# Six of eight output projection tiles per layer as pairs of tiles in seven block products

## The chip, the cores and the metric

The kernel runs on one core of a Trainium2 chip. The metric is device time in microseconds (us) of one execution. The engines are named as in the profile: PE (TensorE, matmuls), PEld (its weight loads), DVE (VectorE), ACT (ScalarE), POOL (GpSimd) and SP (SyncE, which issues nearly all DMAs here). "L996" is line 996 of the kernel before.

## What is computed

The reference is a trunk of two layers over 16 learned meta tokens and 512 sequence tokens (528 in all), 1024 features wide, in float32. One layer is:

```
h = rmsnorm(x)
u_pool, z_pool, c_q, c_kv, k_rope, z_mla, g_pool, g_mla = split(h @ w_in)
y_pool = (pool_mix(u_pool) * silu(z_pool)) @ pool_w_up
y_mla  = (mla(c_q, c_kv, k_rope) * silu(z_mla)) @ mla_w_up
merged = sigmoid(g_pool) * y_pool + sigmoid(g_mla) * y_mla
x = x + merged @ w_out
```

`mla` is latent attention with eight heads, with query blocks of 128 tokens. The output is x without the meta positions. The change touches the last line, `merged @ w_out`, a product of 1024 x 1024 weights with 528 tokens (512 in the last layer).

## The kernel before, in words

Features lie on the 128 partitions and tokens along the columns. Every projection is cut into tiles of 128 output features. A tile is a `Gemm` in the list `plan`; `register` (L1007) writes that list by hand, layer by layer, and `stream` (L190) walks through it as a generator. The layer's own code (`go`, and the attention code in `head`, `prep` and `pv`) draws from that generator in small steps, so that matmuls of the projections fill the gaps of the attention. `after(LAG, fn)` puts a piece of work some modelled nanoseconds later into the stream. The Tile framework then places the instructions of every engine in an order of its own, by their order of emission and by what it holds to be ready, and each engine runs its list in order. So a DMA that is emitted later may stand ahead of an earlier one that has to wait.

Precision is kept by splitting: each float32 operand becomes a high part and a low part in the matmul's own format, and `mm3` (L180) issues three matmuls, high by high, high by low and low by high (L181 to L183). A weight chunk of 512 columns (four blocks of 128 input features for one output tile) is fetched by `fetch` (L114) into `raw`, its high part is made by ACT (L176) and its low part by DVE (L177) in `wload`. There are three buffers each for `raw`, `whi` and `wlo`; a Gemm marked `spare` takes two buffers `th` and `tl` of another pool instead. The stream asks for one chunk ahead of the one it multiplies.

The stretch around the change, in each layer:

- `pu` and `gp` leave the gated pool branch in `am[m]`, which lies in `xb[:, m]`.
- `mu0` to `mu7` are the up-projection of the attention branch, 12 matmuls per chunk of columns. Their evacuation `ev_mu` (L975) takes the PSUM result times the gate into a `tmp` (DVE, L980), adds `am[m]` (POOL, L982) and splits the sum into `mg[m]`, high part on ACT (L275), low part on DVE (L276). `mg[m]` uses the buffers of `h` (`hh`, `hl`).
- `o0` to `o7` are the output projection: for each tile two weight chunks of four input blocks each. `ev_o` (L986) fetches the residual (L990 or L993), adds half of the PSUM result to it (DVE, L996) and stores it (L1000 or L1002); in layer 0 it also squares the new x for the next layer's norm (`square_x`: ACT L347, sums on POOL L351).

Layer 0 works on all 528 tokens in two halves of 264 columns (`FULL`), layer 1 on the 512 sequence tokens in one piece (`XTOK`), but for its last tile, which is cut into halves of 256. PSUM has four tiles `mm`, three `S` and one `o`. The residual tiles `tmp` have three buffers.

Of the kernel before, what the change touches and what calls it, by code (L numbers as in the profile page):

```python
# [71 lines left out]
def trunk(ctx, tc, xT, xrow, mrow, pos, win, wkr, wqb, wkb, wvb, wgr, wpu, wmu, wout, gains, const, yT):  # L72
# [13 lines left out]
    def nm(s):  # L86
        uid[0] += 1
        return f"{s}_{uid[0]}"
# [73 lines left out]
    class Gemm:  # L162
        def __init__(self, name, src, width, evac=None, xs=None, segs=None, body=None):
            self.name, self.src, self.width, self.alloc = name, src, width, mmt
            self.evac, self.xs, self.segs, self.body = evac, xs, segs, body
            self.spare = False

    loads = [0]

    def wload(src, n, spare):  # L170
        raw = early.pop(0) if early else fetch(src, n, rawt(), sp)
        loads[0] += 1
        pool, th, tl, nb = (tp, "th", "tl", 2) if loads[0] <= 2 or spare else (wp, "whi", "wlo", 3)
        hi = pool.tile([P, W if pool is tp else 512], F32R, tag=th, name=nm("whi"), bufs=nb)
        lo = pool.tile([P, W if pool is tp else 512], F32R, tag=tl, name=nm("wlo"), bufs=nb)
        act.activation(hi[:, :n], raw[:, :n], AF.Copy)  # L176
        dve.tensor_sub(lo[:, :n], raw[:, :n], hi[:, :n].bitcast(F32))  # L177
        return hi, lo

    def mm3(out, wh, wl, xh, xl, start, stop):  # L180
        first = pe.matmul(out, wh, xh, start=start, stop=False)  # L181
# [8 lines left out]
    def stream():  # L190
# [4 lines left out]

        def load(i):
            g_, c = flat[i]
            n = min(512, g_.width - c)
            return wload(g_.src[:, c:c + n], n, g_.spare)

# [116 lines left out]
    class Layer:  # L317
        def __init__(self, l):
            self.l, self.last = l, l == DEPTH - 1
            self.XS = XTOK if self.last else FULL  # L320
            self.x0 = NM if self.last else 0
            self.xt = xt if l == 0 else [None] * 8
            self.hs, self.us, self.zps = hbuf, [None] * 4, [None] * 4
            self.cs, self.cqs, self.ys, self.am = [None] * 2, [None] * 6, [None] * 4, [None] * 8
            self.kn, self.qn, self.zms, self.ogs = [None] * 4, [None] * 4, [None] * 4, [None] * 4
            self.qr, self.qf = [None] * 2, [None] * 2
            self.gms, self.mg, self.xr, self.vw = [None] * 8, [None] * 8, [None] * 8, []
            self.made = [None] * 8
            self.csq, self.xsq = [None] * 2, [None] * 8
            self.sq = []  # L330
            self.hosted = self.st = self.acc = self.inv = self.cinv = self.kraw = self.kp = None

        def g(self, c):
            return gn[:, self.l * N_GAIN + c:self.l * N_GAIN + c + 1]
# [640 lines left out]
        def ev_mu(self, m):  # L975
            def ev(ps, a, b):
                if a == self.x0:
                    self.mg[m] = self.hs[m]
                t = tmp()
                dve.scalar_tensor_tensor(out=t[:, :b - a], in0=self.gms[m][:, a:b], scalar=1.0, in1=ps,  # L980
                                         op0=ALU.add, op1=ALU.mult)
                gp.tensor_add(t[:, :b - a], t[:, :b - a], self.am[m][:, a:b])  # L982
# [24 lines left out]
        def register(self, nxt):  # L1007
# [209 lines left out]
```

## Time and profile before

| what | value |
|---|---|
| time, median of three runs | 770.56 us (770.43 to 770.70) |
| span of the profiled execution, first to last instruction | 768.5 us |
| PE busy | 763.8 us, 5195 matmuls |
| DVE busy | 544.1 us, 1179 instructions |
| ACT busy | 408.9 us, 892 instructions |
| POOL busy | 201.6 us, 251 instructions |
| bytes moved by DMA | 84.05 MB |

The profile is of one further execution, for which the page gives the span; the three timed runs lie some 2 us above it, which is what an execution spends before its first and after its last instruction. A busy time is the union of an engine's instructions. The window view gives the busy time of each engine in a stretch of the span; a group row gives the busy time of one kind of instruction and the mean of one in ns; a row of the timeline gives start and duration in us, and in brackets how long the engine had been idle and what ended that. Matmuls are pipelined: a row of PE shows one matmul's duration, while the next one starts much earlier, so the pace is read from the distance of two starts.

### The profile page before, as it was taken

The numbers are of one execution on the slowest core, as the hardware profiler recorded it, in microseconds if no ns is written. First come the engines' busy times: TensorE is split into PE (matmuls) and PEld (weight loads), VectorE is DVE, ScalarE is ACT, GpSimd is POOL, SyncE is SP. The second block draws the span as 40 slices with busy tenths as digits, with TensorE's granted clock in tenths as the row PEclk, the third lists the DMA queues.
The fourth block names the chain that finished last, engine by engine and source line by source line (L and its number), as shares of the span: only waits on it lengthen the run. The fifth ranks groups of instructions, "written<-read, shape, count | busy, mean of one in ns | idle before, by whom it ended". The sixth has DMA issues, their size and how long they took to land.

```text
span 768.5 us, 14355 instructions
## 1 busy us (share of the span) xinstructions
PE 763.8 (99%) x5195; PEld 697.9 (91%) x5195; DVE 544.1 (71%) x1179; ACT 408.9 (53%) x892; POOL 201.6 (26%) x251
## 2 busy tenths in 40 slices
PE   9999999999999999999999999999999999999998
PEld 9999999999999999999997898887888888888887
DVE  5588687357899977785376486773677989775842
ACT  6755656545556665634264355454446666664320
POOL 2026204012242233052220262040132434420500
PEclk9999999999999999999999999999999999999999
DMA  8533233343223222325642333334433332222372
GB/s 293 160 113 98 75 97 98 104 141 105 89 79 91 84 71 70 107 71 169 178 133 97 110 86 89 96 87 127 125 119 90 94 93 77 82 69 70 119 222 98
DMA packets 54931, 84.05 MB, mean 109 GB/s; under 512 B 10006, under 2 KB 18582, under 8 KB 54860
## 3 DMA queue, kind: packets, MB, share of 16 engines
q1 hardware_dynamic: 54716, 82.87, 35.6%
q8 instruction: 41, 0.67, 0.4%
q14 instruction: 30, 0.25, 0.1%
q10 hardware_dynamic: 144, 0.26, 0.1%
HBM read 76.69 MB, written 4.29 MB: 105 GB/s over the span
## 4 chain that ended last, share of the span: by engine, by line
PE 99%; DMA 0%; ACT 0%; DVE 0%; SPq 0%; issue 0%; ACTq 0%
PE mm L181 29%; PE mm L183 29%; PE mm L182 29%; PE mm L859 2%; PE S L181 2%; PE S L182 2%; PE S L183 2%; PE o L876 1%; PE o L872 1%; PE S L503 1%; PE S L470 0%; DMA xb<-xT 0%; PE S L806 0%; PE mm L922 0%; PE mm L395 0%; PE S L872 0%
## 5 line engine op out<-in xcount | busy, mean ns | idle before, releaser
L181 PE MATMUL mm<-hh,whi 128*128 128x264 f32 (+2 forms) x1080 | 339.9, 317 | 0.0
L182 PE MATMUL mm<-hl,whi 128*128 128x264 f32 (+2 forms) x1080 | 338.2, 314 | 0.0
L183 PE MATMUL mm<-hh,wlo 128*128 128x264 f32 (+2 forms) x1080 | 337.1, 315 | 0.0
L177 DVE TENSOR_TENSOR wlo<-raw,whi 128x512 fp32r<-128x512 f32 (+2 forms) x251 | 186.7, 748 | 98.6 <-ACT whi L176 94.6
L176 ACT ACTIVATE whi<-raw 128x512 fp32r<-128x512 f32 (+2 forms) x251 | 150.2, 602 | 181.3 <-PE mm L182 135.3
L181 PEld LDWEIGHTS mm<-hh,whi 128*128 128x128 f32 x1080 | 202.5, 188 | 12.9 <-ACT kp L474 0.4
L182 PEld LDWEIGHTS mm<-hl,whi 128*128 128x128 f32 x1080 | 203.0, 188 | 12.2
L183 PEld LDWEIGHTS mm<-hh,wlo 128*128 128x128 f32 x1080 | 201.9, 188 | 12.2
L743 POOL TENSOR_TENSOR tmp<-kp,bc 64x528 f32<-64x528 f32 x16 | 25.6, 1600 | 123.9 <-PE mm L183 70.0
L604 POOL TENSOR_TENSOR racc<-racc,tmp 128x264 f32<-128x264 f32 (+1 forms) x15 | 14.3, 956 | 133.1 <-ACT tmp L603 133.1
L832 POOL TENSOR_TENSOR pm<-pa,rs 128x16 f32<-128x16 f32 x32 | 9.1, 285 | 126.1 <-DVE rs L827 126.1
L982 POOL TENSOR_TENSOR tmp<-tmp,xb 128x264 f32<-128x264 f32 (+1 forms) x24 | 26.9, 1138 | 56.0 <-DVE tmp L980 55.9
L774 DVE CUSTOM_DVE_ANT_0 S<-S,maskw,nqs 128x400 f32<-128x400 f32 (+4 forms) x80 | 38.4, 499 | 4.4 <-PE S L183 4.0
L781 ACT ACTIVATE cq<-S,bia 128x400 f32<-128x400 f32 (+2 forms) x48 | 24.6, 516 | 27.1 <-DVE bia L774 18.1
L181 PE MATMUL mm<-u,whi 128*128 128x264 f32 (+1 forms) x108 | 34.7, 322 | 0.0
L181 PE MATMUL mm<-cq,whi 128*128 128x264 f32 (+1 forms) x108 | 34.7, 321 | 0.0
L183 PE MATMUL mm<-u,wlo 128*128 128x264 f32 (+1 forms) x108 | 34.7, 321 | 0.0
L183 PE MATMUL mm<-cq,wlo 128*128 128x264 f32 (+1 forms) x108 | 34.5, 321 | 0.0
L182 PE MATMUL mm<-cq,whi 128*128 128x264 f32 (+1 forms) x108 | 34.5, 321 | 0.0
L834 POOL TENSOR_TENSOR cq<-cq,rs 128x384 f32<-128x384 f32 (+1 forms) x32 | 32.8, 1024 | 0.0
L276 DVE TENSOR_TENSOR tl<-mm,th 128x384 fp32r<-128x384 f32 (+1 forms) x48 | 27.9, 596 | 5.0 <-ACT th L275 4.8
L275 ACT ACTIVATE th<-mm 128x384 fp32r<-128x384 f32 (+1 forms) x48 | 24.1, 523 | 10.2 <-PE mm L859 9.2
(270 smaller groups left out, 1378.6 us busy)
## 6 DMA issues: line engine op xcount, KB each, us to landing
raw<-win SPq DMA_DIRECT2D x143, 256.0 KB, 2.6
raw<-wout SPq DMA_DIRECT2D x32, 256.0 KB, 3.0
bc<-kdr SPq DMA_DIRECT2D x16, 264.0 KB, 3.6
raw<-wpu SPq DMA_DIRECT2D x16, 256.0 KB, 2.7
raw<-wmu SPq DMA_DIRECT2D x16, 256.0 KB, 2.7
raw<-wqb SPq DMA_DIRECT2D x12, 256.0 KB, 2.6
xb<-xT SPq DMA_DIRECT2D x8, 264.0 KB, 5.7
tmp<-xT SPq DMA_DIRECT2D x16, 132.0 KB, 3.4
```

What stands on the lines that cost most here:

```text
L176: act.activation(hi[:, :n], raw[:, :n], AF.Copy)
L177: dve.tensor_sub(lo[:, :n], raw[:, :n], hi[:, :n].bitcast(F32))
L181: first = pe.matmul(out, wh, xh, start=start, stop=False)
L182: pe.matmul(out, wh, xl, start=False, stop=False)
L183: newest[0] = pe.matmul(out, wl, xh, start=False, stop=stop)
L275: act.activation(hi[:, a:b], src, AF.Copy)
L276: return dve.tensor_sub(lo[:, a:b], src, hi[:, a:b].bitcast(F32))
L743: gp.tensor_mul(kf[r0:r0 + 64, :], self.kp[r0:r0 + 64, :], bc[r0:r0 + 64, :])]
L774: return dve.tensor_tensor_reduce(out=sv, in0=sv, in1=mask, scale=nqs[:, i, h:h + 1], scalar=3e38, op0=ALU.add, op1=ALU.min, accum_out=bia ...
L781: act.activation(pv, sv, AF.Exp, scale=-1.0, bias=bia[:, i:i + 1], accum_out=rs[:, c:c + 1])
L834: gp.tensor_mul(pt[i][:, NM:], pt[i][:, NM:], rs[:, i:i + 1].to_broadcast([P, n - NM]))
L982: gp.tensor_add(t[:, :b - a], t[:, :b - a], self.am[m][:, a:b])
```

## The change

Tiles o0 and o1 stay as they are. Tiles 2 to 7 are taken as three pairs, (2, 3), (4, 5) and (6, 7). A pair is a product of a 2 x 2 block matrix of weights (two tiles by two halves of the input features) with a 2 x 2 block matrix of tokens (two halves of the input features by two halves of the tokens). Done plainly that is eight block products of four input blocks each, times the three matmuls of the split. Strassen's scheme, in the variant with shared sums, does it with seven, on sums and differences of the blocks:

- Token sums: `combine(w, k)` makes four combined operands (w = 1 to 4) for each of the four k, once per layer, from the float32 values that `ev_mu` now leaves in `am`. Sums w = 1 and 2 are made on POOL, 3 and 4 on DVE; each is then split by ACT and DVE. They are emitted 2000 modelled ns after the second half of `mu` m has been evacuated: w = 1 for m < 4, w = 2, 3, 4 for k = m - 4.
- Weight sums: `pair_operand(p)` loads the four chunks of a pair by DMA into free buffers of the layer (q0 to q3 or cq0 to cq3), makes four sums on POOL and gives seven operands, each split by ACT and DVE (in pairs 2 and 3 the low part of the fourth on POOL), in turns into `whi`/`wlo` and `th`/`tl`.
- Products: `pair_body(p)` runs 12 matmuls of half the tokens per product, into three PSUM tiles A, B and C. B is accumulated over products 1, 3, 5 and 7 and C over 4 and 6; after each product its present sum is added to the residual with weight 0.5 or -0.5, which gives the four blocks.
- `ev_mu` writes the gated sum into `am` in place of the `tmp`.

The diff, cut to its core:

```diff
+    def parts(raw, n, spare, eng):
+        pool, th, tl, nb = (tp, "th", "tl", 2) if spare else (wp, "whi", "wlo", 3)
...
+        act.activation(hi[:, :n], raw[:, :n], AF.Copy)
+        eng.tensor_sub(lo[:, :n], raw[:, :n], hi[:, :n].bitcast(F32))
+        return hi, lo
...
         def load(i):
             g_, c = flat[i]
+            if g_.operand is not None:
+                return g_.operand(c // 512)
...
-                gp.tensor_add(t[:, :b - a], t[:, :b - a], self.am[m][:, a:b])
-                split(*self.mg[m], t[:, :b - a], a, b)
+                f = self.am[m][:, a:b]
+                gp.tensor_add(f, t[:, :b - a], f)
+                split(*self.mg[m], f, a, b)
+                if b == T:
+                    after(LAG, lambda: [self.combine(w, m % 4) for w in ((1,) if m < 4 else (2, 3, 4))])
...
+        def combine(self, w, k):
...
+            f = self.tf[w, k] = sqt()[:, :n]
+            eng = gp if w < 3 else dve
+            if w == 1:
+                eng.tensor_sub(f, lo[:, a0:b0], lo[:, a1:b1])
+            elif w == 2:
+                eng.tensor_add(f, hi[:, a1:b1], self.tf[1, k])
+            elif w == 3:
+                eng.tensor_sub(f, hi[:, a1:b1], lo[:, a1:b1])
+            else:
+                eng.tensor_sub(f, self.tf[2, k], hi[:, a0:b0])
...
+            act.activation(th, f, AF.Copy, scale=sign)
+            dve.scalar_tensor_tensor(out=tl, in0=f, scalar=sign, in1=th.bitcast(F32), op0=ALU.mult, op1=ALU.subtract)
+
+        def pair_operand(self, p):
+            tags = (("cq0", "cq1", "cq2", "cq3", "kn0", "kn1"), ("q0", "q1", "q2", "q3", "kn2", "racc"))[p % 2]
...
+                if i == 0:
+                    for tag, (m, c) in zip(tags, ((0, 0), (0, 512), (1, 0), (1, 512))):
+                        t[m, c] = slot(tag)[:, 0:512]
+                        sp.dma_start(t[m, c], wout[self.l, 2 * p + m, :, c:c + 512])
...
+                    gp.tensor_add(s1, a21, a22)
+                    gp.tensor_add(s2, s1, a11)
+                    gp.tensor_add(a21, a11, a21)
+                    t["all"] = (a11, a12, s2, s1, a21, a12, a22)
+                if i == 5:
+                    gp.tensor_add(t[0, 512], t["all"][2], t[0, 512])
+                return parts(t["all"][i], 512, i % 2 == 1, gp if i == 3 and p > 1 else dve)
...
+        def pair_body(self, p, nxt):
...
+                if i == 0:
+                    product(B, w, quarter(0, a0, b0), True)
+                    add(m1, a0, b0, B, 0.5, False)
+                elif i == 1:
+                    product(A, w, quarter(4, a0, b0), True)
+                    add(m1, a0, b0, A, 0.5, True)
+                elif i == 2:
+                    product(B, w, ts(2), False)
+                    add(m1, a1, b1, B, 0.5, False)
+                elif i == 3:
+                    product(C, w, ts(1), True)
+                    add(m2, a1, b1, C, -0.5, False)
+                elif i == 4:
+                    product(B, w, ts(3), False)
+                    add(m2, a1, b1, B, -0.5, True)
+                elif i == 5:
+                    product(C, w, quarter(4, a1, b1), False)
+                    add(m1, a1, b1, C, 0.5, True)
+                else:
+                    product(B, w, ts(4), False)
+                    add(m2, a0, b0, B, -0.5, True)
...
-            for m in range(8):
-                add(f"o{m}", wout[l, m], D, evac=self.ev_o(m, nxt), xs=mg,
-                    segs=[(NM, NM + SEQ // 2), (NM + SEQ // 2, T)] if self.last and m == 7 else XS)
+            for m in range(2):
+                add(f"o{m}", wout[l, m], D, evac=self.ev_o(m, nxt), xs=mg, segs=XS)
...
+            for p in range(1, 4):
+                add(f"o{2 * p + 1}", None, 7 * 512, body=self.pair_body(p, nxt))
+                plan[-1].operand = self.pair_operand(p)
```

`quarter(k0, a, b)` takes four blocks of `mg`, `ts(w)` the four combined operands; `add` is the DVE addition to the residual, with the store of the finished half behind it.

More of the change, by code (lines that the diff above doesn't have):

```diff
@@ L172, in wload @@
         loads[0] += 1
[L173 to L178, printed above, removed]
+        return parts(raw, n, loads[0] <= 2 or spare, dve)
     def mm3(out, wh, wl, xh, xl, start, stop):
@@ L331, in __init__ @@
             self.hosted = self.st = self.acc = self.inv = self.cinv = self.kraw = self.kp = None
+            n = (T - self.x0) // 2
+            self.HV = [(self.x0, self.x0 + n), (self.x0 + n, T)]
+            self.tf, self.ts = {}, {}
         def g(self, c):
```

56 lines of the change are left out of this document (55 added, 1 removed).

## The prediction

> **What bounds the kernel now.** I read the page first (busy shares, slices, the chain that ended last), then the windows of the two stages that the edit touches, then single rows for the price of one instruction.
>
> ```profile
> span 768.5 us, 14355 instructions
> ...
> PE 763.8 (99%) x5195; PEld 697.9 (91%) x5195; DVE 544.1 (71%) x1179; ACT 408.9 (53%) x892; POOL 201.6 (26%) x251
> ...
> DVE  5588687357899977785376486773677989775842
> ...
> POOL 2026204012242233052220262040132434420500
> PEclk9999999999999999999999999999999999999999
> ...
> PE 99%; DMA 0%; ACT 0%; DVE 0%; SPq 0%; issue 0%; ACTq 0%
> ```
>
> TensorE (PE) is busy for 763.8 of 768.5 us at a granted clock of nine tenths or more in every slice, and 99% of the chain that ended last is PE. So a matmul that is left out is time saved, as long as nothing that feeds PE takes its place. The DVE row warns: it stands at 8 and 9 in the slices around the gate stage of layer 0, and POOL, at 26% over the span, is far busier there than on the mean.
>
> The next rows cut each layer into the end of the up-projection (`mu`, where the gated sum `mg` is built), the tiles o0 and o1, and the tiles o2 to o7.
>
> ```profile
> core 0: us, PE busy (x) PEld busy (x) DVE busy (x) ACT busy (x) POOL busy (x), PEclk, DMA share, GB/s
> 329.40:346.10 16.70, 16.70 (x139) 16.70 (x139) 16.20 (x29) 7.90 (x18) 11.52 (x13) 1.00 0.27 79
> 346.10:357.80 11.70, 11.70 (x99) 11.70 (x98) 7.92 (x15) 4.57 (x9) 3.06 (x4) 1.00 0.49 145
> 357.80:393.40 35.60, 35.60 (x295) 35.60 (x294) 16.10 (x28) 14.60 (x25) 5.32 (x4) 1.00 0.61 179
> 708.90:720.40 11.50, 11.50 (x52) 9.31 (x51) 11.50 (x13) 5.68 (x10) 8.02 (x5) 1.00 0.29 92
> 720.40:731.50 11.10, 11.10 (x49) 9.00 (x48) 8.82 (x13) 3.71 (x7) 4.26 (x3) 1.00 0.48 145
> 731.50:765.20 33.70, 33.59 (x169) 28.13 (x167) 11.22 (x19) 6.30 (x10) 0.00 (x0) 1.00 0.53 165
> ```
>
> PE has no gap in any of them (0.11 us in the last). In the `mu` stage DVE is busy for 16.20 of 16.70 us (layer 0) and 11.50 of 11.50 us (layer 1), and POOL for 11.52 and 8.02. Under o2 to o7 both have room: DVE works 16.10 of 35.60 us and 11.22 of 33.70.
>
> **What the change removes.** Rows of the additions that close a tile or half a tile give PE's pace.
>
> ```profile
> 362.37 0.43 DVE L996 SCALAR_TENSOR_TENSOR xb<-mm,tmp 128x264 f32<-128x264 f32 x1 [0.18 <-PE mm L183]
> ...
> 368.23 0.43 DVE L996 SCALAR_TENSOR_TENSOR xb<-mm,tmp 128x264 f32<-128x264 f32 x1 [0.17 <-PE mm L183]
> ```
>
> ```profile
> 748.36 0.69 DVE L996 SCALAR_TENSOR_TENSOR tmp<-mm,tmp 128x512 f32<-128x512 f32 x1 [1.65 <-PE mm L183]
> ...
> 753.90 0.69 DVE L996 SCALAR_TENSOR_TENSOR tmp<-mm,tmp 128x512 f32<-128x512 f32 x1 [1.65 <-PE mm L183]
> ...
> 763.71 0.42 DVE L996 SCALAR_TENSOR_TENSOR tmp<-mm,tmp 128x256 f32<-128x256 f32 x1 [3.57 <-PE mm L183]
> 765.13 0.42 DVE L996 SCALAR_TENSOR_TENSOR tmp<-mm,tmp 128x256 f32<-128x256 f32 x1 [0.99 <-PE mm L183]
> ```
>
> In layer 0 one tile follows the other every 368.23 - 362.37 = 5.86 us: 48 matmuls of 264 columns, 0.122 us each. In layer 1 24 matmuls of 512 columns take 753.90 - 748.36 = 5.54 us (0.231 each), and 12 of 256 columns take 765.13 - 763.71 = 1.42 us (0.118 each). A block product is 12 matmuls of 264 or 256 columns: 1.465 or 1.42 us. Layer 0 runs 21 of them in place of 24 and saves 3 x 1.465 = 4.4 us. Layer 1 spent 5 x 5.54 + 4 x 1.42 = 33.4 us on o2 to o7 and spends 21 x 1.42 = 29.8 us: 3.6 us less, since narrow matmuls cost a little more per column. Together **8.0 us**. That narrow matmuls hide their weight loads is shown by the 264-column rows, which have a load each.
>
> **What it adds, per layer.** By the diff: 16 combined token operands (`combine`), each one sum (8 on POOL, 8 on DVE), one ACT copy and one DVE subtraction, so 24 DVE, 8 POOL and 16 ACT instructions of half width; four POOL sums of 512 columns per pair; seven weight splits per pair in place of four, one of them on POOL in pairs 2 and 3; 21 additions of half width from PSUM where 12 of 264 columns (layer 0) or five of 512 and two of 256 (layer 1) stood. The unit prices, from rows where nothing else disturbs the instruction:
>
> ```profile
> 348.94 0.42 DVE L276 TENSOR_TENSOR hl<-tmp,hh 128x264 fp32r<-128x264 f32 x1
> 349.29 0.42 DVE L980 SCALAR_TENSOR_TENSOR tmp<-cq,mm 128x264 f32<-128x264 f32 x1
> ```
>
> ```profile
> 727.87 0.68 DVE L276 TENSOR_TENSOR hl<-tmp,hh 128x512 fp32r<-128x512 f32 x1
> 728.47 0.68 DVE L177 TENSOR_TENSOR wlo<-raw,whi 128x512 fp32r<-128x512 f32 x1
> ```
>
> ```profile
> 338.43 0.81 POOL L982 TENSOR_TENSOR tmp<-tmp,xb 128x264 f32<-128x264 f32 x1 [1.38 <-DVE tmp L980]
> ...
> 359.17 1.33 POOL L351 TENSOR_TENSOR cq<-cq,cq 128x528 f32<-128x528 f32 x1 [8.46 <-ACT cq L347]
> ```
>
> A DVE split of 264 columns frees the engine after 349.29 - 348.94 = 0.35 us, one of 512 after 728.47 - 727.87 = 0.60 us (256: about 0.34). POOL takes 0.81 us for 264 columns and 1.33 us for 528, so 1.97 ns a column and 0.29 us fixed: 0.79 us for 256 and 1.30 us for 512. The same straight line through DVE's two gives 0.08 us fixed. But these prices do not hold when the two engines work together:
>
> ```profile
> L276 DVE TENSOR_TENSOR hl<-tmp,hh 128x264 fp32r<-128x264 f32 x16 | 11.3, 720 | 1.2 <-ACT hh L275 1.2
> L980 DVE SCALAR_TENSOR_TENSOR tmp<-cq,mm 128x264 f32<-128x264 f32 x12 | 4.8, 421 | 3.2 <-PE mm L183 3.0
> ```
>
> ```profile
> L982 POOL TENSOR_TENSOR tmp<-tmp,xb 128x264 f32<-128x264 f32 x16 | 14.6, 927 | 27.8 <-DVE tmp L980 27.6
> ```
>
> The split of `hl` reads two SBUF operands and takes 0.720 us on the mean in this stage against 0.42 alone, while the gating instruction L980, which reads PSUM for one operand, stays at 0.421. So POOL passes and DVE instructions with two SBUF operands hold each other up; a DVE instruction with a PSUM operand is not touched. Combined operands, weight splits and POOL sums are all of the kind that is.
>
> The Trainium skill, "SBUF — State Buffer", section "SBUF: two separate sides", states that such a DVE instruction and a GpSimd instruction exclude each other for their whole length. By that rule whole durations add up, which is the upper ledger below; the stretched `hl` and the untouched L980 agree with it in kind.
>
> **Where it meets the path.** PE can run o0, o1 and the first two products on `mg` alone. The third product needs the operands of `combine(2, k)`, and by the order of emission 20 of the 24 added DVE instructions (all for k = 0 to 2, and the first two for k = 3) stand ahead of it, most of them ahead of the last `mg` split. DVE is in order, so the wait may also show up earlier, as late `mg` splits under o0 and o1; the sum is the same. Weight buffers (three of `whi`, two of `th`) keep PE from running further ahead. The times of this stage are the first matmul of o0 in each layer, and the first and last instructions of DVE and POOL that the ledger below counts:
>
> ```profile
> 346.07 0.29 PE L181 MATMUL mm<-hh,whi 128*128 128x264 f32 x1
> ```
>
> ```profile
> 720.38 0.39 PE L181 MATMUL mm<-hh,whi 128*128 128x512 f32 x1
> ```
>
> ```profile
> 329.42 1.11 DVE L980 SCALAR_TENSOR_TENSOR tmp<-cq,mm 128x264 f32<-128x264 f32 x3 [2.98 <-PE mm L183]
> 330.44 2.04 DVE L177 TENSOR_TENSOR wlo<-raw,whi 128x512 fp32r<-128x512 f32 x2
> ```
>
> ```profile
> 351.20 0.43 DVE L276 TENSOR_TENSOR hl<-tmp,hh 128x264 fp32r<-128x264 f32 x1 [0.20 <-ACT hh L275]
> ...
> 352.68 0.69 DVE L177 TENSOR_TENSOR wlo<-raw,whi 128x512 fp32r<-128x512 f32 x1 [0.26 <-ACT whi L176]
> ```
>
> ```profile
> 708.91 4.70 POOL L982 TENSOR_TENSOR tmp<-tmp,xb 128x512 f32<-128x512 f32 x3 [22.64 <-DVE tmp L980]
> ```
>
> ```profile
> 709.28 1.47 DVE L177 TENSOR_TENSOR wlo<-raw,whi 128x512 fp32r<-128x512 f32 x1
> ...
> 727.26 0.68 DVE L177 TENSOR_TENSOR wlo<-raw,whi 128x512 fp32r<-128x512 f32 x1
> ```
>
> Layer 0: work on the pair of engines begins at 329.42; o0 starts at 346.07; the third product would be due at 346.07 + 2 x 5.86 + 2 x 1.465 = 360.7. That is 31.3 us. Due in it: POOL 16 gate sums, 8 combined sums and 2 weight sums, 16 x 0.81 + 8 x 0.81 + 2 x 1.30 = 22.0 us; DVE with two SBUF operands 16 splits, 20 added, 8 weight splits (from the one at 330.44 to the one at 352.68) and 3 for the pair, 36 x 0.35 + 11 x 0.60 = 19.2 us. One after the other they need 41.2 us: 9.9 us late. If only the parts that grow with the columns exclude each other (0.52 and 1.01 us on POOL, 0.27 and 0.52 on DVE) they need 29.9 us: not late.
>
> Layer 1: from 708.91 to 720.38 + 2 x 5.54 + 2 x 1.42 = 734.3 there are 25.4 us. POOL 8 x 1.30 + 8 x 0.79 + 2 x 1.30 = 19.3; DVE 8 x 0.60 + 20 x 0.34 + 10 x 0.60 = 17.6 (seven weight splits from 709.28 to 727.26, three for the pair). Whole: 36.9, 11.5 us late. Columns only: 28.7, 3.3 us late.
>
> Today the same ledger gives for layer 0, up to the last `mg` split at 351.20 + 0.43, 16 x 0.81 + 16 x 0.35 + 6 x 0.60 (six weight splits stand ahead of it) = 22.2 us (whole) or 15.8 (columns only), and it took 351.63 - 329.42 = 22.2. That would speak for whole durations, but part of that time PE, which supplied `mu` until 346.07, set the pace. So I take the middle: 4.3 us late in layer 0 and 7.4 in layer 1.
>
> **The pairs themselves.** A pair in layer 0 holds up to 5 x 1.30 us of POOL sums and splits, 5 sums of squares over three pairs (1.67 x 1.33), and 6 DVE weight splits (3.6 us): 12.3 us whole, 9.9 columns only, against 7 x 1.465 = 10.3 us of PE. Late by 2.0 or 0, middle 0.9, three times: 2.6 us. In layer 1, without squares: 10.1 or 8.1 against 9.9, so 0 to 0.2 each; I take 0. The four combined instructions for k = 3 that are left fall beside products 3 to 6 and cost nothing in the middle ledger; whole, they are 4 x 0.35 = 1.4 us a layer, inside the upper end's slack.
>
> **Edits at nothing.** The additions read PSUM and fit (7 x 0.35 = 2.5 us a pair on a DVE that now idles over half of that stage). ACT has 16 half copies more, by an estimate as long as DVE's 0.35 us, beside 4.57 of 11.70 us busy under o0 and o1. The gate sum written in place frees `tmp` one step earlier, worth at most DVE's 0.5 us of waits in the `mu` window. Weight DMAs move the same bytes:
>
> ```profile
> raw<-wout SPq DMA_DIRECT2D x32, 256.0 KB, 3.0
> ```
>
> They land in 3.0 us; pair 1's four are free to go when `mu` has released q0 to q3, two tiles (11 us) before use. Without that cover, if SP held them behind a store that waits for a product, each pair would start some 3 us late; in the page SP already issues `wout` loads ahead of earlier stores, so I count none. A stalled `tmp` would hold the residual load, needed only from product 3 on. The last addition and store stay as they are.
>
> **Sum.** Late: 4.3 + 7.4 + 2.6 = 14.3 us; saved 8.0; net +6.3 us. The three runs' median, 770.56, stands 2.1 us above the profiled span of 768.5, and I add the net to the median: **776.9 us**. Bounds: 3.3 - 8.0 gives 765.9; 9.9 + 11.5 + 6.1 + 0.5 = 28.0 late gives 790.6.
>
> **Rivals.** *Faster (0.33):* the passes of POOL and DVE mostly run side by side. Place: the 31.3 and 25.4 us ahead of the third product. Then only DVE's own line counts, 19.2 us plus 21 instructions from PSUM of 0.35 (7.4), 26.6 of 31.3 us in layer 0, and 17.6 + 6.3 = 23.9 of 26.2 us (from DVE's own start at 708.07) in layer 1. Nothing is late and the time goes to 762.6; with the lower ledger 765.9. It decides below 8.0 us late in all, a sixth of the way from the lower ledger to the upper. For it: PE has no gap in the windows above although DVE ends its last `mg` split 5.6 us after `mu` (351.63 against 346.07), and the order is free to use any gap. Against: the 0.720 us row.
> *Whole exclusion (0.17):* both engines add up everywhere, 783 to 791 us, 790.6 by the ledger. For it: the layer 0 stage of today, 22.2 us by its ledger and 22.2 measured. Against: POOL's gate sums, too, would be stretched about as far as DVE's splits, and they take 0.927 us on the mean against 0.81. The rule of the Trainium skill named above speaks for this case.
> *Even (0.08):* lateness of 6.5 to 9.5 us cancels the saving.
> *The change saves no PE time (under 0.01, in none of the above):* excluded by the 1.42 us row.
>
> **Numbers.** The forecast, 772 to 784, has 0.42. I call 0.2% (1.5 us) what a measurement of this kernel can tell from no change. Faster 0.33, same 0.08, slower 0.42 + 0.17 = 0.59. The range runs from 764 to 790: it takes in the lower ledger and nearly all of the upper, and leaves out about 0.06 below and 0.06 above.
>
> **What would show it.** Right: PE gaps of 3 to 8 us in each layer between o0 and the third product, ended by a DVE split (of a combined operand, a weight or `mg`) and not by a DMA; half-width subtractions at 0.5 to 0.9 us; PE busy down by about 8 us. Wrong: combined subtractions near 0.43 us with PE still at 99% (faster); PE waiting for DMA or for PSUM additions in pairs 2 and 3 (another mechanism).

## The result, and the profile after

The changed kernel takes **803.27 us** (median of 4 runs, 802.37 to 803.53) against 770.57 for the kernel before beside it: a ratio of 1.042 (95% interval 1.041 to 1.044), 32.7 us slower. The forecast was 776.9 us with a range from 764 to 790: the sign was right, the size far out.

The page of the changed kernel, the lines that answer to those of before:

```profile
PE 771.2 (96%) x5243; PEld 703.7 (88%) x5243; DVE 606.5 (76%) x1264; ACT 430.5 (54%) x942; POOL 259.4 (32%) x295
...
DVE  5588677557899977799876576675588899668994
...
POOL 2026103013333311574620262030223442307831
PEclk9999999999999999997999999999999999999699
...
PE 85%; DVE 9%; DMA 2%; issue 1%; ACT 0%; POOL 0%; SPq 0%; DVEq 0%; ACTq 0%
```

PE is now off the chain for 15% of it, and DVE stands in its place (9%). The granted clock, nine tenths or more everywhere before, falls to 7 and 6 in the two slices of the output projections. PE busy went *up* by 7.4 us where 8.0 us of matmuls were left out: what is left took 15.4 us more. By an estimate some 10.5 us of this is the lower clock (PE's busy time in windows of 1 us, each times the share of the clock that was missing); where the other 4.9 went I have not traced.

The span of its profiled execution is 801.4 us. The windows of the changed kernel, in the columns of the windows of before and cut at its own marks. The first product of a pair starts at 374.28 and 747.28, the third in layer 1 at 766.90.

```profile
346.10:357.80 11.70, 8.04 (x52) 7.52 (x52) 11.70 (x16) 5.36 (x13) 9.52 (x10) 0.85 0.29 100
357.80:374.28 16.48, 10.09 (x52) 9.04 (x51) 16.48 (x27) 4.62 (x11) 9.76 (x8) 0.69 0.22 71
374.28:412.00 37.72, 34.87 (x278) 33.91 (x277) 30.42 (x48) 20.69 (x35) 16.27 (x11) 1.00 0.43 135
...
731.50:747.28 15.78, 13.22 (x50) 10.03 (x49) 15.78 (x17) 5.62 (x13) 13.28 (x11) 0.89 0.38 126
747.28:766.90 19.62, 13.83 (x58) 11.07 (x57) 19.62 (x29) 8.12 (x19) 11.56 (x9) 0.74 0.12 40
766.90:797.90 31.00, 26.93 (x218) 25.73 (x216) 21.18 (x37) 8.90 (x15) 9.84 (x7) 1.00 0.41 132
```

From 346.10 to 374.28 DVE is busy for every us while PE is idle for 10 of 28; before, DVE had room there and PE had no gap. The same pattern stands in layer 1 from 731.50 to 766.90. Behind the third product (last row) the clock is full again and DVE has room.

The PE rows that end the longest gaps, and between them the first matmuls of the first, fourth and third products of pair 1 in layer 0, in the order in which they ran (start, duration, in brackets the gap and what ended it):

```profile
350.00 0.59 PE L184 MATMUL mm<-hh,whi 128*128 128x264 f32 x1 [3.18 <-DVE tmp L988]
...
363.59 0.59 PE L185 MATMUL mm<-hl,whi 128*128 128x264 f32 x1 [2.53 <-DVE hl L281]
...
374.28 0.28 PE L1053 MATMUL mm<-hh,whi 128*128 128x264 f32 x1
...
377.21 0.41 PE L1053 MATMUL mm<-u,whi 128*128 128x264 f32 x2
...
379.42 0.48 PE L1053 MATMUL mm<-kh,whi 128*128 128x264 f32 x2 [0.58 <-DVE tmp L1059]
...
752.64 0.58 PE L1053 MATMUL S<-hh,wlo 128*128 128x256 f32 x1 [3.69 <-DVE wlo L175]
```

The gaps are ended by DVE instructions, as forecast, though the first of them by the gating instruction and not by a split. The third product (`kh`, `kl`) was due at 360.7 and starts at 379.42: 18.7 us late. In layer 1 it was due at 734.3, or 750.5 with the 16.2 us that the whole layer starts later, and starts at 766.90: 16.4 late. That is 35.1 us of lateness. Not all of it is lost: the framework ran the fourth product (`u`) ahead of the third in both layers, 1.5 and 1.4 us of work that PE has to do anyway. So of the 32.7 + 8.0 = 40.7 us that were lost, 32.2 were lost ahead of the third product and 8.5 in the pairs behind it.

Why DVE is full: its groups in layer 0 from 330 to 374.3, by line and shape (count, busy us, mean ns):

```profile
L281 DVE TENSOR_TENSOR hl<-xb,hh 128x264 fp32r<-128x264 f32 x16 | 12.0, 761 | 0.0
L175 DVE TENSOR_TENSOR wlo<-raw,whi 128x512 fp32r<-128x512 f32 x7 | 8.0, 1139 | 0.0
L988 DVE SCALAR_TENSOR_TENSOR tmp<-cq,mm 128x264 f32<-128x264 f32 x12 | 4.9, 419 | 3.1 <-PE mm L186 3.1
L1010 DVE TENSOR_TENSOR sq<-sq,xb 128x264 f32<-128x264 f32 x4 | 3.9, 969 | 0.0
...
L1016 DVE SCALAR_TENSOR_TENSOR kh<-sq,kh 128x264 fp32r<-128x264 f32 x2 | 3.1, 1526 | 0.0
```

and POOL's in the same stretch, the gate sums and the longest and the shortest of seven weight sums:

```profile
L991 POOL TENSOR_TENSOR xb<-tmp,xb 128x264 f32<-128x264 f32 x16 | 15.1, 957 | 26.5 <-DVE tmp L988 25.8 <-DMA q<-wout 0.7
...
L1031 POOL TENSOR_TENSOR cq<-cq,cq 128x512 f32<-128x512 f32 x1 | 1.8, 1754 | 0.0
...
L1029 POOL TENSOR_TENSOR kn<-q,q 128x512 f32<-128x512 f32 x1 | 1.5, 1453 | 0.0
```

DVE instructions with two SBUF operands are stretched: a 512 split from 0.68 to 1.14 us on the mean, a 264 split to 0.76, some splits of token operands to 1.5 (alone 0.42). The gating instruction, which reads PSUM, keeps its 0.42. POOL's 512 sums take up to 1.75 us. And POOL makes seven weight sums in this stretch, where the forecast had counted two: three of pair 2, which run first, and four of pair 1. Once the last of them has ended, at 368.98, DVE's splits are back at 0.42 and 0.68. Rows of POOL and of DVE:

```profile
367.50 1.48 POOL L1034 TENSOR_TENSOR q<-racc,q 128x512 f32<-128x512 f32 x1
```

```profile
369.54 0.42 DVE L281 TENSOR_TENSOR hl<-xb,hh 128x264 fp32r<-128x264 f32 x1
...
370.23 0.68 DVE L175 TENSOR_TENSOR wlo<-q,whi 128x512 fp32r<-128x512 f32 x1
```

### The profile page after: what moved, and what is told of

It reads as the page before. It is cut to its first block, busy times and chain, and to the rows that moved or that the text cites. A ratio compares the mean times of both kernels' runs of the same rounds, so it can differ in the third digit from the quotient of the medians.

```text
span 801.4 us, 14631 instructions
## 1 busy us (share of the span) xinstructions
PE 771.2 (96%) x5243; PEld 703.7 (88%) x5243; DVE 606.5 (76%) x1264; ACT 430.5 (54%) x942; POOL 259.4 (32%) x295
## 4 chain that ended last, share of the span: by engine, by line
PE 85%; DVE 9%; DMA 2%; issue 1%; ACT 0%; POOL 0%; SPq 0%; DVEq 0%; ACTq 0%
PE mm L184 23%; PE mm L186 23%; PE mm L185 23%; PE mm L1053 4%; DVE wlo L175 3%; PE mm L867 2%; PE S L184 1%; PE S L185 1%; PE S L186 1%; DVE hl L281 1%; PE o L884 1%; PE o L880 1%; PE S L511 1%; DVE tmp L988 1%; DMA xb<-xT 1%
## 5 line engine op out<-in xcount | busy, mean ns | idle before, releaser
L185 PE MATMUL mm<-hl,whi 128*128 128x264 f32 (+1 forms) x928 | 293.9, 318 | 7.6 <-DVE hl L281 7.6
L184 PE MATMUL mm<-hh,whi 128*128 128x264 f32 (+1 forms) x928 | 295.1, 320 | 5.5 <-DVE tmp L988 4.0
L186 PE MATMUL mm<-hh,wlo 128*128 128x264 f32 (+1 forms) x928 | 292.1, 318 | 1.4 <-DVE wlo L175 1.4
L175 DVE TENSOR_TENSOR wlo<-raw,whi 128x512 fp32r<-128x512 f32 (+2 forms) x227 | 172.9, 765 | 76.4 <-ACT whi L174 75.0
L174 ACT ACTIVATE whi<-raw 128x512 fp32r<-128x512 f32 (+2 forms) x227 | 135.0, 599 | 135.8 <-PE mm L185 92.6
L185 PEld LDWEIGHTS mm<-hl,whi 128*128 128x128 f32 x928 | 176.3, 190 | 19.5 <-DVE hl L281 9.1
L184 PEld LDWEIGHTS mm<-hh,whi 128*128 128x128 f32 x928 | 175.6, 190 | 18.1 <-DVE tmp L988 4.9
L186 PEld LDWEIGHTS mm<-hh,wlo 128*128 128x128 f32 x928 | 175.3, 190 | 12.4 <-DVE wlo L175 1.7
L991 POOL TENSOR_TENSOR xb<-tmp,xb 128x264 f32<-128x264 f32 (+1 forms) x24 | 27.6, 1160 | 51.6 <-DVE tmp L988 50.9
L789 ACT ACTIVATE cq<-S,bia 128x400 f32<-128x400 f32 (+2 forms) x48 | 24.6, 516 | 27.1 <-DVE bia L782 18.4
```

The source lines that it names most:

```text
L175: eng.tensor_sub(lo[:, :n], raw[:, :n], hi[:, :n].bitcast(F32))
L185: pe.matmul(out, wh, xl, start=False, stop=False)
L186: newest[0] = pe.matmul(out, wl, xh, start=False, stop=stop)
L789: act.activation(pv, sv, AF.Exp, scale=-1.0, bias=bia[:, i:i + 1], accum_out=rs[:, c:c + 1])
L991: gp.tensor_add(f, t[:, :b - a], f)
```

## Experiments

Each experiment ran beside the kernel before, whose time was 770.49 to 770.79 us in all of them. "Mark" is a point just behind layer 0: the start of layer 1's matmuls for `k_rope`, right behind its norm sums on PE (before 411.18, changed 427.38).

**Which of the added operands costs.** e1 and e2 leave out one kind of sum, e3 both; the products are as many. First the edit of e1 and e3, then that of e2 and e3:

```diff
-                if b == T:
-                    after(LAG, lambda: [self.combine(w, m % 4) for w in ((1,) if m < 4 else (2, 3, 4))])
-                ts = lambda w_: [self.ts[w_, k] for k in range(4)]
+                ts = lambda w_: quarter(4 * (w_ % 2), a1, b1)
```

```diff
-                    gp.tensor_add(s1, a21, a22)
-                    gp.tensor_add(s2, s1, a11)
-                    gp.tensor_add(a21, a11, a21)
-                    t["all"] = (a11, a12, s2, s1, a21, a12, a22)
+                    t["all"] = (a11, a12, a21, a22, a21, a12, a22)
...
-                    gp.tensor_add(t[0, 512], t["all"][2], t[0, 512])
```

> Leaves out the 16 combined token operands of each layer (their sums, copies and subtractions); the products read halves of mg in their place, so the output is not the reference's. Exclusion (whole durations of POOL passes and of DVE instructions with two SBUF operands add up): the stage ahead of the third product loses 24 x 0.35 + 8 x 0.8 = 14.8 us per layer, 803.3 - 29 = 774 us. DVE alone is the limit (POOL does not matter): only 24 x 0.35 = 8.4 us per layer, 786 us.

> Leaves out the 12 POOL sums of weights per layer (the products read the plain chunks, so the output is not the reference's); all DVE and ACT instructions stay. Exclusion: the seven sums that run in the stage ahead of the third product go, 7 x 1.3 = 9.1 us per layer, and some 2 us in the pairs: 803.3 - 22 = 781 us. DVE alone: no change, 800 to 804 us.

> Leaves out token operands and weight sums (output not the reference's); seven products per pair, their 21 additions and seven weight splits stay. If the cost lies in the sums and operands: 762 to 766 us, the saving of 8.0 us nearly whole. If the products themselves are dearer than 12 matmuls (weight splits too slow, accumulation waits): above 770 us.

e1 777.39 us (ratio 1.009), e2 785.74 (1.020; its two runs are 783.88 and 787.60), e3 768.94 (0.9985, interval 0.9975 to 0.9996). e1 and e2 come nearer to the exclusion cases than to the others; e3 falls between its two cases. Over e3 the token operands alone (e2) cost 16.8 us, the weight sums alone (e1) 8.5, both together 34.3: some 9 more than one by one. And e3 itself has none of the sums and gains 1.6 us of the 8.0. The products are as fast as forecast (in its chain of waits, layer 1):

```profile
750.37 9.94 PE mm L1045 x84
```

That is seven products in 9.94 us, 1.42 each. In layer 0 the saving of 4.4 us is all given back (mark 411.26). PE's longest gaps there, 3.1 us in all:

```profile
363.57 0.36 PE L1045 MATMUL mm<-hh,whi 128*128 128x264 f32 x1 [1.27 <-ACT whi L174]
...
390.11 0.36 PE L1045 MATMUL mm<-hh,whi 128*128 128x264 f32 x1 [0.97 <-ACT hh L348]
393.14 0.39 PE L185 MATMUL mm<-hl,whi 128*128 128x264 f32 x1 [0.82 <-DVE hl L350]
```

The first gap waits for a weight split; a product uses up a chunk in 1.46 us where a plain tile needs 2.9. The other two wait for the next layer's `h`, which hangs on the last additions. Shortening PE's part only uncovers them.

**Is it POOL against DVE, or DVE alone?** e4 moves all sums of the change from POOL to DVE, e5 the 16 gate sums too, so that POOL stands still in the stage and DVE does it all. The last two lines are e5's alone:

```diff
-            eng = gp if w < 3 else dve
+            eng = dve
-                    gp.tensor_add(s1, a21, a22)
+                    dve.tensor_add(s1, a21, a22)
...
-                gp.tensor_add(f, t[:, :b - a], f)
+                dve.tensor_add(f, t[:, :b - a], f)
```

> All sums that the change put on POOL (8 token sums, 12 weight sums and two low parts per layer) run on DVE instead; the gate sums stay on POOL. Exclusion: in the stage POOL loses 8 x 0.8 + 7 x 1.3 = 15.5 us and DVE gains 8 x 0.35 + 7 x 0.60 = 7.0 us per layer, 803.3 - 17 = 786 us, and lone DVE splits return to 0.42 and 0.68 us outside the gate sums. DVE alone: 7 us more per layer, 817 us.

> As the run before with all sums of the change on DVE, and the gate sums of mu (16 of 264 columns, 8 of 512) on DVE as well, so POOL has nothing to do in the stage. Exclusion: what POOL held for 16 x 0.81 or 8 x 1.30 us becomes 16 x 0.35 or 8 x 0.60, about 6.5 us less per layer, 793.4 - 13 = 780 us, and no DVE split of 264 columns over 0.45 us is left in the stage. DVE alone: 5 us more per layer, 804 us.

e4 793.44 us (1.030), e5 789.23 (1.0245): with *more* work on the engine that is full, 9.8 and 14.0 us faster than the change. Both lie between their two cases, nearer to exclusion. e5's groups and its window of the stretch:

```profile
L281 DVE TENSOR_TENSOR hl<-xb,hh 128x264 fp32r<-128x264 f32 x16 | 6.6, 417 | 0.0
...
L175 DVE TENSOR_TENSOR wlo<-raw,whi 128x512 fp32r<-128x512 f32 x7 | 4.8, 679 | 0.0
```

```profile
330.00:374.30 44.30, 37.21 (x291) 35.71 (x290) 43.33 (x109) 22.18 (x50) 0.00 (x0) 1.00 0.42 136
```

With POOL idle every split is back at 0.42 and 0.68 us: POOL's passes are what stretched them. But DVE alone is still busy for 43.33 of 44.30 us, now with 109 instructions where the changed kernel got 69 done, and e5 stays 18.4 us above before. Both theories hold a part: the hold-up makes POOL's help worth less than nothing here, and with all of it on one engine the amount alone still makes the change slower.

**Is it the place?** e6 puts pair 1's weight sums behind the last token sum and pair 2's behind the third product's addition; f1 makes every token sum and each pair's first weight sum wait for the layer's last `mg` split, and emits the token operands together there. The edits of e6 and of f1:

```diff
+                    if p == 1:
+                        follow(made, self.token_sum)
+                    elif p == 2:
+                        behind(made, self.third)
```

```diff
+                if b == T and m == 7:
+                    self.release = made
+                    self.combine_all()
...
+            behind(made, self.release)
...
-                    gp.tensor_add(s1, a21, a22)
+                    behind(gp.tensor_add(s1, a21, a22), self.release)
```

> Only the order of POOL changes: pair 1's weight sums stand behind the last token sum, pair 2's behind the first addition of the third product. If the weight sums that ran ahead of need are a term of the lateness: three to five of them leave the stage, 4 to 6.5 us per layer, 790 to 795 us, part of it given back in the pairs. If they are not (POOL had the time anyway): 802 to 804 us.

> The whole change, all three pairs in both layers, but the sums of the 16 token operands and the first weight sum of each pair wait for the last mg split of the layer, so nothing of them can stand ahead of o0 and o1's own operands. If the loss comes from where the added instructions stand (between the mg splits), o0 and o1 run as before, the wait moves to the third product, whose operands then have some 9 (layer 0) and 12 us (layer 1) for some 14 to 20 us of work: 5 to 10 and 3 to 8 us late, and with the waits of the pairs, 6 to 9 us, and the saving of 8.0 the time is 777 to 790 us. If the amount of work before the third product alone sets the loss, whatever its order, the time stays at 800 us or more.

e6 800.89 us (1.039), f1 804.52 (1.044). e6 falls between its two cases. In it the third product of layer 0 starts 3.7 us earlier than in the changed kernel (375.73), but the last product ends 1.0 later (its last matmul starts at 411.96 against 410.95): in layer 0 what is taken out ahead of the pairs comes back in them, and 2.4 us remain in all. f1 gains nothing. f1's windows and its longest gap in layer 0:

```profile
346.10:357.80 11.70, 11.57 (x95) 11.36 (x94) 8.14 (x14) 4.71 (x12) 8.43 (x9) 1.00 0.55 171
357.80:384.00 26.20, 13.99 (x66) 11.09 (x65) 24.53 (x38) 9.97 (x22) 19.40 (x15) 0.64 0.32 102
```

```profile
375.97 0.59 PE L1059 MATMUL mm<-u,whi 128*128 128x264 f32 x1 [3.94 <-DVE u L1022]
```

o0 and o1 now run without a gap of note, and the wait stands at the token operands (`u`, of the fourth product); the mark is 426.46 against 427.38. With three pairs it does not help to move the sums behind the `mg` splits: what is won in o0 and o1 is lost at the first pair. f1 came out as in its last case, 800 us or more: the place alone is not what made the whole change slow.

**One pair.** e9 takes only tiles 6 and 7 as a pair, so the combined operands are due some 23 us later; e10 does that in layer 1 alone and asks for the token operands 16000 modelled ns later. The edits of e9 and of e10 (without its conditions for the layer):

```diff
-            for m in range(2):
+            for m in range(6):
-            for p in range(1, 4):
+            for p in range(3, 4):
```

```diff
-                    after(LAG, lambda: [self.combine(w, m % 4) for w in ((1,) if m < 4 else (2, 3, 4))])
+                    after(LAG + 16000.0, lambda: [self.combine(w, m % 4) for w in ((1,) if m < 4 else (2, 3, 4))])
```

> Tiles o0 to o5 of both layers stay plain; only tiles 6 and 7 are a pair, with the same token operands, emitted at the same place as in the changed kernel. It saves at most 1.46 us in layer 0 and 1.28 in layer 1, and the first use of a combined operand is due some 23 us later than in the changed kernel. If only that due time matters (the forecast's account: the work has to be done ahead of the third product) the cover of o2 to o5 hides all of it: 768 to 770 us. If the added instructions delay the mg splits and weight splits that they stand ahead of, whatever they are needed for, the tiles o0 to o2 come late all the same and PE shows gaps there: 775 to 783 us.

> Layer 0 is as before the change. In layer 1 only tiles 6 and 7 are a pair, and the token operands are emitted 16000 modelled ns later, so that they lie beside o2 to o4, where DVE works a third of the time. Saved: 1.28 us. If the price of the change is that its sums stand ahead of the work that PE needs next, nothing is late and the time is 769.0 to 769.6 us. If the sums and splits cost time wherever they are put, over 772 us.

e9 795.96 us (1.032), e10 783.86 (1.017), both far above the covered case, and e9 above its other case too. PE rows of e9 and of e10:

```profile
365.15 0.59 PE L185 MATMUL mm<-hl,whi 128*128 128x264 f32 x1 [5.41 <-DVE hl L281]
```

```profile
740.18 0.80 PE L185 MATMUL mm<-hl,whi 128*128 128x512 f32 x1 [3.78 <-DVE hl L281]
```

PE waits inside o0 and o1 for an `mg` split (`hl`). The framework put token subtractions (`sq`), which nothing needs yet, between the `mg` splits, in e10 too: emitting them later did not move them. DVE ahead of e10's gap:

```profile
736.11 1.48 DVE L1010 TENSOR_TENSOR sq<-sq,xb 128x256 f32<-128x256 f32 x1
737.51 1.48 DVE L1008 TENSOR_TENSOR sq<-xb 128x256 f32<-128x256 f32 x1
738.92 1.21 DVE L281 TENSOR_TENSOR hl<-xb,hh 128x512 fp32r<-128x512 f32 x1
```

So f2 and f3 tie them by a dependence: in layer 1 behind the addition of o1, in f3's layer 0 behind the last `mg` split. f4 has two pairs in layer 1, tied behind the addition of o0. The edit of f2, in `ev_o` and in `combine`:

```diff
+                if self.last and m == 1:
+                    self.release = made
+                    self.combine_all()
...
+            behind(made, self.release)
```

> As e10 (layer 0 as before, one pair of tiles 6 and 7 in layer 1), but the token sums and the first weight sum wait for the addition of o1 to the residual, so that they must lie beside o2 to o5. If e10 was slow only because its sums were placed among the mg splits, this gives 769.0 to 769.8 us, as DVE and POOL have 20 us for 8 us and 13 us of work; with the engines excluding each other, up to 2 us more. If the sums cost the same wherever they are, 780 us or more.

> The same in both layers: one pair, tiles 6 and 7. In layer 1 the sums wait for the addition of o1, in layer 0 for the last mg split (o0's addition overwrites a block that they read, so they cannot wait for that). Saved at most 2.74 us. If place is all that matters: 767.8 to 769.5 us. If the operands of layer 0 still come into the way of o0 and o1: 772 to 778. If the sums cost the same wherever they are: about 795, as e9.

> Layer 0 as before; in layer 1 the pairs (4, 5) and (6, 7), with the token sums and the first weight sums waiting for the addition of o0. Saved at most 2.4 us. The third product of the first pair is due some 17 us after the sums may start, for which POOL has 16.8 us of passes and DVE 8.2 us beside its own weight splits. Hidden: 768.2 to 769.5 us. One after the other: 5 to 10 us late, 773 to 779.

f2 776.63 us (1.007, interval 1.0055 to 1.009), f3 783.76 (1.017), f4 780.16 (1.012). f2 and f3 fall between their cases, f4 just above its late one. Against e10 and e9 the tie is worth 7.2 of 13.1 and 12.2 of 25.2 us: for one pair the place is about half of the loss. f4's two pairs lose more than f2's one: less cover for more work. What is left in f2, by windows and the row behind the gap:

```profile
728.00:759.00 31.00, 30.83 (x150) 25.76 (x151) 27.58 (x46) 14.42 (x32) 15.11 (x13) 1.00 0.42 143
759.00:762.00 3.00, 0.56 (x5) 0.38 (x4) 1.19 (x3) 0.63 (x1) 0.00 (x0) 1.00 0.55 175
762.00:766.00 4.00, 4.00 (x23) 4.00 (x23) 1.04 (x3) 0.00 (x0) 0.00 (x0) 0.59 0.11 37
```

```profile
761.84 0.36 PE L1056 MATMUL mm<-hh,whi 128*128 128x256 f32 x1 [2.44 <-DVE tmp L1062]
```

All sums lie under o2 to o5, and PE is busy for 30.83 of 31.00 us: hidden. Then PE waits for an addition that waits for the residual's load, which waits for a `tmp` buffer and so for an older store; and behind the gap the clock is 0.59 over 4 us. The low clock did not come in every run: in two of f2's six the mean clock stayed at 1.00, and they took 774.4 and 774.5 us, the other four 776.4 to 778.7. By an estimate from these times it is worth some 2 us or more, and the wait itself the 1.3 that are left to f5's 773.2. f5 gives the pair's residual tiles free buffers, f6 also keeps the seven products in the order of the source (the last line, at each matmul of a product).

```diff
-                        st["x", m] = tmp()
+                        st["x", m] = slot(f"cq{4 + m - m1}")
...
+                        follow(made, newest[0])
```

> f2 (one pair in layer 1, sums behind o1's addition) with the pair's two residual tiles in buffers that the gates have left free, so that their loads no longer wait for a tmp buffer and the stores behind it. In f2 PE had a gap of 2.45 us at 761.8, ended by an addition that had waited for that load, and a granted clock of 0.59 in the 4 us behind it (some 1.6 us). If that wait is the price, and the low clock its consequence, both go: 772 to 773 us, PE clock 1.00. If the clock falls for another reason, 774 us with the low clock still there.

> f5 with the seven products held in the order of the source on PE. In f2 the framework drew products together that add into the same PSUM tile, and PE waited 0.61 us twice for the addition in between. If these waits come from that order, they go: 1.2 us below f5, 770 to 771.5 us. The whole saving of one pair is 1.28 us, so at best 769.3, just below the kernel before.

f5 773.19 us (1.003, interval 1.002 to 1.004), f6 772.60 (1.0018, interval 1.0009 to 1.0027): f5 just above its range (772 to 773), f6 above its own (770 to 771.5). The gap and the low clock went together (the clock is 1.00 in f5), as expected; the order was worth 0.6 by the medians, where I expected 1.2 and where the two intervals overlap. In f6's trace the two waits of 0.61 us are gone, and PE has waits for weight splits of 0.48 and 0.74 us in their place. f6 is the best full version, and it is still 1.9 us slower than before. **No kernel that makes all the operands beat the one before.**

**Two side questions.** e7 adds two matmuls after each k of o0 and o1, to hold the clock up.

> After each k of o0 and o1 two extra matmuls into an unused PSUM tile (7.8 and 7.4 us of PE per layer, results unused), so that PE is idle less and the granted clock should stay at 1.0 in the stage. If the halved clock costs time on the path: up to 6 us per layer come back, 791 to 797 us. If DVE sets the end of the stage and the slow matmuls only use up its lateness: 800 to 807 us.

It took 808.99 us (1.048), 5.7 more than the change; its mean clock rose only from 0.982 to 0.989, and it was still 0.84 from 346 to 374, so it does not settle what the low clock costs where DVE is full anyway. It lies above both of its cases.

m1 and m2 add 18 unused POOL sums of 512 columns to the kernel before.

> The kernel before with 18 POOL sums of 512 columns beside o1 to o6 of layer 1, on tiles that nothing else reads. Exclusion for whole durations: weight splits that meet a sum take 0.69 us plus up to a sum's 1.3 us (1.2 to 1.9), the additions from PSUM stay at 0.69, sums that meet a split take 1.3 + 0.45 us; the time stays within 1 us of 770.5. Exclusion for the growing part only: splits stretch to at most 1.7 us and sums hardly. None: all at 0.69 and 1.3.

> The kernel before with 18 POOL sums of 512 columns added that nothing uses, three behind each addition of o1 to o6 in layer 1, where POOL was idle. Nothing waits for them. If POOL passes and DVE instructions with two SBUF operands hold each other up, a weight split that meets a sum takes 1.2 to 1.9 us in place of 0.68, the additions from PSUM keep 0.69, and the time stays within 1 us of the kernel before. If the two engines work side by side, the splits keep 0.68.

m1's sums had no tie and ran at 647 to 687 us, beside another stage than meant: 771.99 us (1.0014), 1.2 us slower. m2's are tied to the additions of o1 to o6: 770.72 us (0.9999). The DVE groups of before and of m2, from 715 to 768 us:

```profile
L177 DVE TENSOR_TENSOR wlo<-raw,whi 128x512 fp32r<-128x512 f32 x16 | 12.0, 754 | 9.6 <-ACT whi L176 9.6
```

```profile
L177 DVE TENSOR_TENSOR wlo<-raw,whi 128x512 fp32r<-128x512 f32 x16 | 14.3, 901 | 9.6 <-ACT whi L176 9.6
...
L996 DVE SCALAR_TENSOR_TENSOR tmp<-mm,tmp 128x512 f32<-128x512 f32 x7 | 4.8, 692 | 7.2 <-PE mm L183 7.1
```

Splits that meet a sum are stretched (to 1.17 us in the rows of o1 to o3, the low end of what was expected), additions from PSUM are not, and where DVE has room it costs nothing.

## Why the forecast was right in sign and wrong in size

- **Saved, 8.0 us: right as a pace, wrong as a gain.** In layer 1 of e3 1.42 us a product was measured, but only 1.6 of 8.0 us reaches the end when no sum is made at all.
- **The place of the wait: right.** PE gaps of up to 3.2 and 3.7 us in the two layers up to the third product, ended by DVE; stretched half-width subtractions, some beyond the 0.9 us forecast; PSUM readers untouched. "PE busy down by about 8 us" failed: it rose by 7.4, in the main since the clock fell.
- **Late ahead of the third product, 4.3 + 7.4 = 11.7 us: the step that failed; measured 35.1, of which 32.2 are lost.** The step counted two weight sums on POOL and 20 added DVE instructions ahead of it, by the order of emission. The order that ran is the framework's: ahead of the *first* product of layer 0 already stand seven weight sums (pair 2's too), all 24 token instructions of DVE and 10 weight splits. With these counts POOL needs 16 x 0.81 + 8 x 0.81 + 7 x 1.30 = 28.5 us and DVE 40 x 0.35 + 10 x 0.60 = 20.0: 48.5 us whole, 35.6 columns only, 42.0 in the middle, where the forecast's middle was 35.5. It took 374.28 - 330.00 = 44.3 us, two thirds of the way. So the 18.7 us of layer 0 come apart:

| part of the lateness in layer 0 | us |
|---|---|
| forecast | 4.3 |
| the count: 42.0 in place of 35.5 | 6.5 |
| the exclusion nearer to whole: 44.3 in place of 42.0 | 2.2 |
| the first two products, which the forecast let PE run meanwhile, came only behind all of this | 2.9 |
| the fourth product, run ahead of the third (not lost) | 1.5 |
| an addition that came late, behind the residual's load | 0.7 |
| the stage began later | 0.6 |

The clock is 1.00 between the first and the third product and has no part in these rows; the addition that the third product waits for, at 378.84, had itself waited for `tmp<-xT`, the load of the residual. In layer 1 the same reading gives POOL 8 x 1.30 + 8 x 0.79 + 7 x 1.30 = 25.8 us and DVE 8 x 0.60 + 23 x 0.34 + 11 x 0.60 = 19.2: 45.0 us whole, 35.1 columns only, 40.1 in the middle, where the forecast had 32.8. From POOL's first gate sum (724.96) to the third product it took 41.9. So the count makes some 7 of the 9.0 us by which layer 1 exceeds its forecast of 7.4.

The choice on the exclusion was nearly right; what stands in the window was not. But the count is not a price that comes back when it is cut: e6 cuts it and lets the third product start earlier, f1 lets o0 and o1 go ahead, and the time hardly moves (-2.4 and +1.3 us). As far as these two runs show, the stretch ahead of the third product and the pairs behind it share one budget of DVE and POOL time, and the forecast set the whole of it too small.

- **The pairs, 2.6 us: too small; measured 8.5.** The forecast had the POOL sums and squares of layer 0 here and counted layer 1 as nothing; e3, without any sum, shows waits for weight splits and at the layer's end that it had not, and the residual's load comes on top.
- **An edit counted at nothing that was not: the residual load.** I wrote that a stalled `tmp` would hold it, "needed only from product 3 on", and put no price. Products 3 and 6 add into PSUM tiles that earlier additions have to read first, and these additions need the residual, so it is on the path. In the changed kernel's last pair, SP's issues, the DVE row behind them and PE's row behind that:

```profile
785.06 0.33 SPq L1064 DMA_DIRECT2D yT<-tmp  x1
788.83 0.33 SPq L1077 DMA_DIRECT2D tmp<-scr  x1
```

```profile
792.02 0.76 DVE L1059 SCALAR_TENSOR_TENSOR tmp<-mm,tmp 128x256 f32<-128x256 f32 x2 [3.01 <-DMA tmp<-scr]
```

```profile
792.50 0.39 PE L1053 MATMUL mm<-hh,whi 128*128 128x256 f32 x1 [0.86 <-DVE tmp L1059]
```

A store, then the load into its buffer, then DVE idle for 3.01 us; PE, which still had products to run, waits 0.86 us of it. In the kernel with one pair the load costs more: f2 to f5 prices it at 3.4 us, with the low clock behind it.

- **The rivals.** Whole exclusion came nearest, 790.6, and its ledger was short by the same count. The faster case fell on the hold-up, not on DVE's own line: in layer 0 that line is 20.0 us and 19 instructions from PSUM of 0.35 (6.6), 26.6 of the 44.3 us in which DVE was never idle. The other 17.7 are what POOL's passes, 28.5 us if alone, added to it.

The Trainium skill, "SBUF — State Buffer", section "SBUF: two separate sides", says that of such a pair of instructions the later is blocked for the whole of the other. The trace agrees in kind (e5, and the untouched PSUM readers) and lies below it in size: 44.3 us against 48.5.

What stays open: how much of the roughly 10.5 us of slow matmuls lies on the path. In f2 it does, where DVE had room; in the changed kernel DVE was full beside it, and e7 could not separate the two.

## What to carry to other kernels

Before a product is traded for sums, write down what the vector engines have to do in the very window where the sums fall and in the products behind it, with the count taken from the order that will run and not from the order of emission, and ask what the saving is worth with all sums at nothing (here 1.6 of 8.0 us). Where POOL and DVE both read two SBUF operands, POOL is no second engine: in this stage it was faster to let DVE do everything (789.2 against 803.3 us). Here work that was due late had to be tied by a dependence to stay out of the way; emitting it later was not enough.

## What the runs showed of the hardware that I had not expected

- A gap of 2.44 us on PE, with PE busy ahead of it and behind it, was enough for the granted clock to fall in f2's profiled execution: it is 0.50 in each us from 763 to 766, and 0.59 over the 4 us behind the gap. It does not happen in every run: the mean clock of two of f2's six runs stayed at 1.00. And in f5 a gap of 1.99 us at 729.81 left the clock at 1.00. In the changed kernel the clock is 0.69 over 16 us, and at the halved clock matmuls of 264 columns start 0.22 us apart in place of 0.12:

```profile
364.20 0.42 PE L184 MATMUL mm<-hh,whi 128*128 128x264 f32 x1
364.42 0.42 PE L184 MATMUL S<-hh,whi 128*128 128x264 f32 x1
```

The Trainium skill, "TensorE: Matmul & The Clock Gate", section "Part 1: The HAM clock gate", gives the halved clock and a window of about 3.4 us for it; f2's gap is shorter than that.

- POOL is slowed as well as DVE: a sum of 512 columns took up to 1.75 us, 1.30 by the rows of before.
